# A two-layer decoder trunk on one core: one four-column tile of the base pool gets sixteen columns

## The chip, the cores and the metric

The kernel runs on one core of a Trainium2 chip. The metric is the device time of one execution in microseconds, as the median of several runs. A core has TensorE (PE; its weight loads are listed apart as PEld), VectorE (DVE), ScalarE (ACT), GpSimd (POOL) and SyncE (SP), which here only issues DMAs.

## The reference

The input is one sequence of 512 tokens of width 2048. Two layers follow each other, each with a modulated RMS norm in front and a gated residual add behind, and one RMS norm ends it:

```python
for i in range(DEPTH):                                   # DEPTH = 2
    mod = (c_act @ ada_w[i] + ada_b[i])[:, None, :]
    shift, scale, gate = jnp.split(mod, 3, axis=-1)
    h = rmsnorm(x, norm_g[i]) * (1.0 + scale) + shift
    if i % 2 == 0: y = retention_branch(h, positions, ...)   # 8 heads, dk 256, dv 512
    else:          y = mla_branch(h, positions, ...)         # 16 heads, ranks 512 and 512
    x = x + gate * y
return rmsnorm(x, final_norm_g)
```

The retention branch projects h to q, k (rotary), v and a gate g for 8 heads, forms decayed causal scores in chunks, normalises each head, multiplies by silu(g) and projects back. The attention branch projects h to two latent blocks of 512 (for queries, and for keys and values), one shared rotary key and a gate, expands the latents for 16 heads, does causal softmax attention, multiplies by silu(g) and projects back. All is float32.

## The kernel before

A product of float32 matrices is done as three matmuls on float32r parts: each operand x is split into a high part (a cast on ScalarE) and a low part x - high (a subtraction on VectorE), and high x high, high x low and low x high are added up in PSUM. Each matmul has a stationary operand of 128x128 and a moving operand of 128x512 or 128x256.

Tiles come from pools. The pool `base` lives through the whole kernel. It holds, in this order, the identity, mask and ones, a few columns of constants (`mhalf`, `rt`, `vcol` and six of the modulation), and then large tiles by tag, each tag with a fixed number of buffers: `big` (16 of 4096 bytes a partition), `small` (24 of 32 bytes), `k4` (8 of 4096), `k4b` (4 of 4096), `tmp` (6 of 2048), `raw` (3 of 4096), `whi` and `wlo` (3 of 4096 each). Behind these stand `qn_s` and two tiles of 64 bytes (`mod_c`). A tile takes its bytes of a partition rounded up to a multiple of 32. Behind `base` stands one inner pool at a time, each beginning at the same byte: `l0` in the first stage, `lp` in the stage of the retention heads' projections, `l1` in the retention and its output projection, `l2` in the attention layer.

Work goes in steps written out by hand (`Step`: load, prepare, multiply, follow); the order on each engine's queue is fixed by the program. DMAs of weights are issued on SP three units ahead.

The stage that most concerns the change is that of the heads 1 to 7. For each head the q and k rows are formed by `seven_rows_steps` (for heads 6 and 7 by plain steps), and values and gates by `seven_steps`: two products that share an input are done with seven half-products in the place of eight, over 8 units with four products and 8 units with three. Stationary is a block of h (`hT`, tag `big`) or of sums of its blocks (`sums`: 0 to 7 in `k4`, 8 to 11 in `k4b`, 12 to 15 in the inner pool). Moving is a part of the weights, 512 columns wide; in `seven_rows_steps` it is the other way round, and 256 columns wide. The names of parts: `vg_01o_h` is unit 1 of the first eight, its odd rows, high part; `vg_17e_l` is unit 7 of the second eight, even rows, low part.

Where raw weights and parts are put goes in turn:

```python
turns1 = turns(
    ((lambda: lpp, "own_r", 3), (lambda: base, "raw", 3)),
    ((lambda: lpp, ("own_h", "own_l"), 1), *3 * ((lambda: base, ("whi", "wlo"), 3),)),
)
```

So every second raw tile and every fourth pair of parts stand in `lp` (as `turns2` does in `l2`), the others in `base`. The odd parts of units 1, 3, 5 and 7 of the first eight and the even parts of units 1, 3, 5 and 7 of the second eight are those in `lp`. The product of `seven_steps` (lines 804 to 806 of the profile) is

```python
for b in range(2):
    a = form(n, u, b)
    PE.matmul(banks[b], a[0], w[0], start=first, stop=False, skip_group_check=True)
    PE.matmul(banks[b], a[0], w[1], start=False, stop=False, skip_group_check=True)
    PE.matmul(banks[b], a[1], w[0], start=False, stop=True, skip_group_check=True)
```

The latent rows of the second layer (`vgc_`) go through the same function with `l2` as the inner pool, and two of its gate blocks through `seven_rows_steps` (line 903). In the attention `pt`, the transposed probabilities in parts, stands in `l2` and is the moving operand of the value products. Transposes by TensorE (`yT` L1253, `pT` L1992, `y_ps` L2400) have the identity as one operand. DMAs that land in inner pools are every second raw tile, the modulation weights (`mod`, `aw`, `mod_gate`) and what the retention heads read back.

`qn_s` holds the four columns of one norm's gain, scaled by 192 to the power -1/2. It is written by one instruction of VectorE and read by four of ScalarE and four of VectorE.

Of the kernel before, what the change touches and what calls it, by code (L numbers as in the profile page):

```python
# [9 lines left out]
F32 = mybir.dt.float32  # L10
# [6 lines left out]
P = 128  # L17
T = 512
NT = T // P
# [30 lines left out]
def hybrid_trunk_kernel(  # L50
# [32 lines left out]
    base = ctx.enter_context(tc.tile_pool(name="base", bufs=1))  # L83
# [1654 lines left out]
            DVE.tensor_add(latent["q"][2 + b], m4[b], y_[b])  # L1738
            DVE.tensor_add(latent["kv"][2 + b], m5[b], y_[b])

    qn_s = base.tile([P, NT], F32, name="qn_s")

    def latent_norm(n):
        if n == "q":
# [726 lines left out]
```

## Time and profile before

| | before |
|---|---|
| three timed runs | 2156.14, 2157.33, 2159.07 us |
| median | 2157.33 us |
| the profiled execution: its span, first to last instruction | 2153.4 us |
| mean granted TensorE clock | 0.999 |
| HBM read, written | 417.96 MB, 43.00 MB |

The timed runs are whole executions; the profiled one is a further execution of which the span is known, 3.9 us under the median. A row of the views below names the line of the kernel, the engine, the operation and the tiles as out<-in with buffer numbers left out; x14 is a count. A matmul's duration in a row is longer than the distance between two matmuls' starts, since they are pipelined.

### The profile page before, as it was taken

The page shows a single profiled execution, that of the slowest core. Times are in us where ns is not written, and L with a number is a line of the kernel's source. Part 1 is how long each engine was busy: PE and PEld are TensorE (multiplying, and loading weights), DVE is VectorE, ACT ScalarE, POOL GpSimd, SP SyncE. Part 2 cuts the span into 40 slices and gives each one's busy share as a digit, 9 for nine tenths or more (in the row PEclk, how much of TensorE's full clock was granted, in tenths as well). Part 3 has the DMA queues.
Part 4 walks back from the last instruction along what each step waited for, and adds up shares of the span by engine and source line. Part 5 has one row for each costly group of instructions (what it writes and reads, how often), then busy time and mean ns, then how long its engine had stood idle before and what let it go on. Part 6 is the DMA issues. An engine that isn't in the chain of part 4 may idle for free.

```text
span 2153.4 us, 30041 instructions
## 1 busy us (share of the span) xinstructions
PE 2128.3 (99%) x11100; PEld 1822.8 (85%) x11100; DVE 1676.1 (78%) x2481; ACT 1057.1 (49%) x1604; POOL 106.8 (5%) x178
## 2 busy tenths in 40 slices
PE   7999999999999999999999999999999999999998
PEld 5888898988889888888888888898889989888887
DVE  7899788888878789766777787668978788886755
ACT  5764444444444444434344445345446565664434
POOL 1010000000000000000000000010001000000000
PEclk9999999999999999999999999999999999999999
DMA  9976686877777778765646567553556544346734
GB/s 382 401 278 196 224 273 225 274 239 259 255 258 255 230 235 281 246 206 168 242 158 233 188 215 248 166 171 113 166 178 208 182 137 145 118 135 220 243 109 137
DMA packets 229782, 462.96 MB, mean 215 GB/s; under 512 B 20817, under 2 KB 84337, under 8 KB 225793
## 3 DMA queue, kind: packets, MB, share of 16 engines
q1 hardware_dynamic: 217424, 421.85, 59.4%
q0 software_dynamic: 11920, 38.91, 4.6%
q8 instruction: 87, 1.43, 0.3%
q14 instruction: 61, 0.50, 0.1%
q10 hardware_dynamic: 290, 0.27, 0.0%
HBM read 417.96 MB, written 43.00 MB: 214 GB/s over the span
## 4 chain that ended last, share of the span: by engine, by line
PE 84%; DVE 6%; DMA 5%; issue 2%; ACT 2%; POOL 1%; SPq 0%; POOLq 0%; DVEq 0%; ACTq 0%
PE o L1385 9%; PE o L2307 4%; PE y L805 2%; PE y L806 2%; PE s L805 2%; PE y L804 2%; PE s L806 2%; PE x L806 2%; PE x L805 2%; PE s L804 2%; PE x L804 2%; PE x_qk L903 2%; PE y_qk L903 2%; PE s_qk L903 2%; PE qk L163 2%
## 5 line engine op out<-in xcount | busy, mean ns | idle before, releaser
L1385 PE MATMUL o<-o_h,o_whi 128*128 128x512 f32 (+1 forms) x496 | 192.3, 388 | 0.0
L1385 PE MATMUL o<-o_h,o_wlo 128*128 128x512 f32 (+1 forms) x496 | 191.5, 386 | 0.0
L1385 PE MATMUL o<-o_l,o_whi 128*128 128x512 f32 (+1 forms) x496 | 191.3, 386 | 0.0
L136 DVE TENSOR_TENSOR o_wlo<-o_r,o_whi 128x1024 fp32r<-128x1024 f32 x61 | 74.5, 1224 | 49.0 <-ACT o_whi L135 48.1
L1385 PEld LDWEIGHTS o<-o_h,o_wlo 128*128 128x128 f32 x496 | 93.2, 188 | 19.1 <-DVE o_wlo L136 0.4
L1385 PEld LDWEIGHTS o<-o_h,o_whi 128*128 128x128 f32 x496 | 93.2, 188 | 18.3
L1385 PEld LDWEIGHTS o<-o_l,o_whi 128*128 128x128 f32 x496 | 93.2, 188 | 18.2
L163 PE MATMUL qk<-hT,qk_l 128*128 128x512 f32 x192 | 74.9, 390 | 1.5 <-DVE qk_l L136 1.5
L135 ACT CAST o_whi<-o_r 128x1024 fp32r<-128x1024 f32 x61 | 63.5, 1051 | 25.0 <-PE o L1385 22.0
L356 DVE SCALAR_TENSOR_TENSOR aw<-aw,c_all 128x2048 f32<-128x2048 f32 (+1 forms) x35 | 73.2, 2103 | 2.5 <-DMA aw<-in_ada_t_dram 2.5
L161 PE MATMUL qk<-hT,qk_h 128*128 128x512 f32 x192 | 75.0, 391 | 0.0
L162 PE MATMUL qk<-hT,qk_h 128*128 128x512 f32 x192 | 74.7, 389 | 0.0
L1087 DVE SCALAR_TENSOR_TENSOR mod<-mod,c_odd 128x1024 f32<-128x1024 f32 x48 | 58.1, 1221 | 18.8 <-DMA mod<-in_ada_t_dram 18.8
L136 DVE TENSOR_TENSOR o_w_lo<-o_w_raw,o_w_hi 128x1024 fp32r<-128x1024 f32 x32 | 39.0, 1221 | 32.4 <-ACT o_w_hi L135 32.4
L1087 DVE SCALAR_TENSOR_TENSOR mod<-mod,c_bm 128x1024 f32<-128x1024 f32 x48 | 58.5, 1219 | 0.0
L2307 PE MATMUL o<-o_h,o_w_hi 128*128 128x512 f32 (+1 forms) x160 | 55.6, 348 | 0.0
L2307 PE MATMUL o<-o_h,o_w_lo 128*128 128x512 f32 (+1 forms) x160 | 55.5, 347 | 0.0
L2307 PE MATMUL o<-o_l,o_w_hi 128*128 128x512 f32 (+1 forms) x160 | 55.4, 347 | 0.0
L1240 ACT ACTIVATE yn<-y,nmr,gn_r 128x512 f32<-128x512 f32 x32 | 22.3, 778 | 62.0 <-DVE nmr L1234 62.0
L135 ACT CAST o_w_hi<-o_w_raw 128x1024 fp32r<-128x1024 f32 x32 | 33.5, 1051 | 36.0 <-PE o L2307 32.2
L135 ACT CAST o_h<-o_in 128x1024 fp32r<-128x1024 f32 x24 | 25.2, 1051 | 50.6 <-PE o L162 46.7
L161 PE MATMUL o<-o_h,o_w_hi 128*128 128x512 f32 x128 | 50.1, 391 | 0.0
(1607 smaller groups left out, 6896.6 us busy)
## 6 DMA issues: line engine op xcount, KB each, us to landing
mod<-in_ada_t_dram SPq DMA_DIRECT2D x96, 512.0 KB, 5.8
o_r<-in_ret_w_out_dram SPq DMA_DIRECT2D x64, 512.0 KB, 5.5
aw<-in_ada_t_dram SPq DMA_DIRECT2D x30, 1024.0 KB, 8.9
mod_gate<-in_ada_t_dram SPq DMA_DIRECT2D x32, 512.0 KB, 5.1
o_w_raw<-in_mla_w_out_dram SPq DMA_DIRECT2D x32, 512.0 KB, 4.1
qk_r<-in_ret_w_in_dram SPq DMA_DIRECT2D x48, 256.0 KB, 3.1
qk_r<-qk_d SPq DMA_DIRECT2D x32, 256.0 KB, 6.0
v_r<-v_d SPq DMA_DIRECT2D x32, 256.0 KB, 6.2
```

Of the source, the lines that this page charges most:

```text
L135: ACT.copy(hi, src)
L136: DVE.tensor_sub(lo, src, hi.bitcast(F32))
L161: PE.matmul(o, lhs[0], rhs[0], start=first and not seeded, stop=False, skip_group_check=seeded)
L162: PE.matmul(o, lhs[0], rhs[1], start=False, stop=False, skip_group_check=seeded)
L163: return PE.matmul(o, lhs[1], rhs[0], start=False, stop=last, skip_group_check=seeded)
L804: PE.matmul(banks[b], a[0], w[0], start=first, stop=False, skip_group_check=True)
L805: PE.matmul(banks[b], a[0], w[1], start=False, stop=False, skip_group_check=True)
L806: PE.matmul(banks[b], a[1], w[0], start=False, stop=True, skip_group_check=True)
L903: PE.matmul(o, w[wp][:, i, b * P : (b + 1) * P], a[ap], start=first and i + b + k == 0, stop=k == 2, skip_group_check=True,)
L1087: DVE.scalar_tensor_tensor(out=aw, in0=aw, scalar=1.0, in1=silu_c[j], op0=ALU.mult, op1=ALU.mult, accum_out=mc[:, j, b : b + 1],)
L1385: PE.matmul(o, w[i][:, ki, c0 + b * P : c0 + (b + 1) * P], a[j], start=first and i + j == 0, stop=last and i == 1, skip_group_check=True,)
L2307: PE.matmul(banks2[b][:, cols], w[0][i][:, 0, b * P : (b + 1) * P], o2_moving(w, u, cols)[j], start=u + i + j == 0, stop=u == KD - 1 and i ...
```

## The change

`qn_s` is allocated with 16 columns in the place of 4, and its first four columns are used. It takes 64 bytes of a partition, where it took 16, rounded up to 32. What stands behind it, the two `mod_c` tiles and all inner pools, begins 32 bytes later. No instruction is added, removed or moved.

```diff
-    qn_s = base.tile([P, NT], F32, name="qn_s")
+    qn_s = base.tile([P, 16], F32, name="qn_s")[:, :NT]
```

## The prediction

> **What bounds the kernel now.** I read the page first, then the windows view by stage, then the view of one line (L804) and of single tiles, then the timeline of TensorE.
>
> ```profile
> span 2153.4 us, 30041 instructions
> ...
> PE 2128.3 (99%) x11100; PEld 1822.8 (85%) x11100; DVE 1676.1 (78%) x2481; ACT 1057.1 (49%) x1604; POOL 106.8 (5%) x178
> ...
> PE   7999999999999999999999999999999999999998
> ...
> DMA  9976686877777778765646567553556544346734
> ...
> PE 84%; DVE 6%; DMA 5%; issue 2%; ACT 2%; POOL 1%; SPq 0%; POOLq 0%; DVEq 0%; ACTq 0%
> ```
>
> TensorE is the bound: 2128.3 of 2153.4 us busy, 84% of the chain of waits. A change that adds and removes no instruction can only matter here if TensorE's own instructions get longer or shorter. The profiled execution has a span of 2153.4 us; the median of the three timed runs is 2157.33 us (2156.14 to 2159.07), so I put 3.9 us outside the span and carry a change of the span over to the median one to one. What a measurement of this kernel can tell from no change is about 0.2%, that is 4.3 us.
>
> ```profile
> core 0: us, PE busy (x) PEld busy (x) DVE busy (x) ACT busy (x) POOL busy (x), PEclk, DMA share, GB/s
> ...
> 201.00:284.00 83.00, 83.00 (x365) 67.97 (x364) 65.75 (x82) 39.52 (x48) 4.30 (x8) 1.00 0.75 241
> ...
> 440.00:560.00 120.00, 120.00 (x691) 105.60 (x690) 100.61 (x130) 55.10 (x66) 8.28 (x15) 1.00 0.77 254
> ...
> 1555.00:1625.00 70.00, 70.00 (x310) 57.29 (x309) 50.87 (x62) 31.37 (x38) 0.00 (x0) 1.00 0.61 195
> ```
>
> In the stages that form the retention heads' values and gates (201 to 908 us) and the latent rows (1555 to 1624 us) TensorE has no idle time at all, at full clock, while VectorE is at 0.73 to 0.84 and the DMA engines at 0.61 to 0.77. Whatever a matmul gains or loses in these stages shows in the end.
>
> **Where the tiles begin.** This is arithmetic on the program, not on the chip. A pool lays its tiles one behind another, each rounded up to 32 bytes of a partition. Ahead of the first large tile of the base pool stand, from byte 4224 (a multiple of 64), three tiles of 512, two of 32 (16 rounded up), vcol of 736 and six of 64 bytes: 2720 bytes, so the tag big begins at byte 6944, remainder 32 of 64. The other large tags follow in multiples of 64 and have the same remainder. qn_s (16 bytes, rounded to 32) stands behind them, so the small tiles after it and the inner pools (l0, lp, l1, l2) begin at remainder 0: byte 171712 for the first. With 64 bytes for qn_s everything behind it moves by 32 bytes, and all large tiles stand at remainder 32. [...]
>
> **What the trace shows of it.** In seven_steps the moving operand is a part of the weights. Every fourth pair of parts is taken from the inner pool (own_h, own_l), the others from the base pool (whi, wlo). So one line holds both kinds. The columns are ns min/median/max over the seven heads.
>
> ```profile
> L804 PE MATMUL x<-vg_01e_h,hT x14: 389/389/389, 211.8 to 836.7; 128*128 128x512 f32 x14
> ...
> L804 PE MATMUL z<-vg_01o_h,hT x14: 394/396/398, 214.5 to 839.4; 128*128 128x512 f32 x14
> ...
> L804 PE MATMUL x<-vg_02e_h,hT x14: 389/390/393, 217.3 to 842.2; 128*128 128x512 f32 x14
> ...
> L804 PE MATMUL z<-vg_02o_h,hT x14: 389/389/389, 220.1 to 844.9; 128*128 128x512 f32 x14
> ...
> L804 PE MATMUL s<-vg_06e_h,sums x14: 394/394/394, 240.7 to 865.6; 128*128 128x512 f32 x14
> ...
> L804 PE MATMUL y<-vg_17e_h,sums x14: 387/388/390, 282.2 to 907.0; 128*128 128x512 f32 x14
> ```
>
> vg_01e, vg_02o and hT are base tiles: 389 ns, all fourteen times. vg_01o is an inner tile: 396. vg_02e is a base tile again, but follows right behind the inner one and needs a few matmuls to get back. In s<-vg_06e_h,sums the moving operand is a base tile and the stationary one (sums 12, in lp) an inner one: 394. In y<-vg_17e_h,sums both are inner tiles: 387 to 390, like base tiles that have just been disturbed. So it is the mixing of remainders 0 and 32 that goes with the longer time, in whichever operand. The timeline shows how far apart matmuls start:
>
> ```profile
> 323.73 0.40 PE L804 MATMUL x<-vg_00e_h,hT 128*128 128x512 f32 x1
> ...
> 326.05 0.39 PE L805 MATMUL s<-vg_00e_l,sums 128*128 128x512 f32 x1
> ...
> 329.22 0.39 PE L804 MATMUL x<-vg_01e_h,hT 128*128 128x512 f32 x1
> ...
> 331.94 0.40 PE L804 MATMUL z<-vg_01o_h,hT 128*128 128x512 f32 x1
> ...
> 334.75 0.39 PE L804 MATMUL x<-vg_02e_h,hT 128*128 128x512 f32 x1
> ...
> 400.97 0.40 PE L903 MATMUL x_qk<-hT,qk_00e_h 128*128 128x256 f32 x2
> ```
>
> Twelve matmuls of base tiles take 331.94 - 329.22 = 2.72 us, 226.7 ns each. The twelve with vg_01o take 334.75 - 331.94 = 2.81 us, 234 ns each: 7 ns more, as in the durations.
>
> **The change part by part.** It removes, adds and moves no instruction, DMA or wait; no queue is passed.
>
> Matmuls of 512 columns in seven_steps: one head has 8 units of 4 products and 8 of 3, each of 2 blocks by 3 passes, so (32 + 24) x 6 = 336 matmuls. From 323.73 to 400.97 they take 77.24 us; at 226.7 ns each they would take 76.17 us. The excess is 1.07 us a head. Of it 108 matmuls have one or two inner operands (66 in the first eight units, 42 in the second), at 6 to 7 ns; the rest are base matmuls just behind them. After the change I take all of them at 226.7 ns, except the first ten of a head, which come from the 256-column matmuls of L903 out of step: 323.73 to 326.05, 232 ns each, an excess of 0.05 us that stays. Gain 1.02 us a head. Seven heads and the latent rows (the same function and steps; I take the same excess) make 8 x 1.02 = 8.2 us, all on TensorE without a pause, hidden by nothing. What would be late next is VectorE at 0.84, so nothing waits.
>
> Matmuls of 256 columns (the q and k heads and two gate blocks, seven_rows_steps):
>
> ```profile
> L903 PE MATMUL y_qk<-sums,qk_01o_h x32: 278/280/286, 293.6 to 647.1; 128*128 128x256 f32 x32
> L903 PE MATMUL s_qk<-sums,qk_02e_h x32: 283/283/283, 296.5 to 650.0; 128*128 128x256 f32 x32
> ...
> L903 PE MATMUL y_qk<-sums,qk_03o_h x32: 278/282/283, 302.2 to 655.7; 128*128 128x256 f32 x32
> L903 PE MATMUL s_qk<-sums,qk_03e_h x32: 277/280/282, 303.7 to 657.1; 128*128 128x256 f32 x32
> ```
>
> Here mixing goes the other way: 283 ns with base tiles (qk_02e), 280 to 282 with an inner operand (qk_01o, qk_03o, qk_03e). By the code 96 of a pass's 336 have one, six passes, some 580 matmuls. Matched, I price them at 283: 2 ns each, 1.2 us lost; the bounds are 0 (they keep their time) and 3 ns, 1.7 us.
>
> The attention's value products take pt from the inner pool as moving operand: three 512-column matmuls for each of 16 heads, 48 x 7 ns = 0.3 us at most. I leave it out of the sum and put it in the range.
>
> Transposes read ident, which stands at remainder 0 ahead of all this, with a base tile (x2, L2400) or an inner one (yn, L1253) as the other operand:
>
> ```profile
> L2400 PE MATMUL y_ps<-ident,x x32: 272/272/306, 2139.5 to 2144.5; 128*128 128x128 f32 x32
> ...
> L1253 PE MATMUL yT<-ident,yn x128: 270/272/283, 993.6 to 1364.2; 128*128 128x128 f32 x128
> ```
>
> 272 ns either way: the change, which makes the second like the first, costs nothing here.
>
> VectorE and ScalarE (both vg_01o and vg_02o are read raw from the inner pool, written to inner and to base tiles):
>
> ```profile
> L838 ACT CAST vg_01o_h<-vg_01o_r x7: 1050/1054/1054, 208.0 to 834.6; 128x1024 fp32r<-128x1024 f32 x7
> L839 DVE TENSOR_TENSOR vg_01o_l<-vg_01o_r,vg_01o_h x7: 1219/1226/1226, 209.3 to 835.7; 128x1024 fp32r<-128x1024 f32 x7
> ...
> L838 ACT CAST vg_02o_h<-vg_02o_r x7: 1048/1050/1051, 212.7 to 840.3; 128x1024 fp32r<-128x1024 f32 x7
> L839 DVE TENSOR_TENSOR vg_02o_l<-vg_02o_r,vg_02o_h x7: 1224/1226/1226, 213.8 to 841.4; 128x1024 fp32r<-128x1024 f32 x7
> ```
>
> 1226 against 1226 and 1054 against 1050: the remainder is worth at most 4 ns in 1050, beside work at 0.84 of the stage or less. Nothing.
>
> DMAs that land in inner tiles (mod) against base tiles (o_r), the same 512 KB:
>
> ```profile
> mod<-in_ada_t_dram SPq DMA_DIRECT2D x96, 512.0 KB, 5.8
> o_r<-in_ret_w_out_dram SPq DMA_DIRECT2D x64, 512.0 KB, 5.5
> ```
>
> The base tiles, which have the remainder that all will have, are landed on no slower; between -0.3 us and nothing for a transfer, with TensorE busy beside it. I take 0.
>
> Sum: -8.2 + 1.2 = -7.0 us on the span: 2146.4 us, and 2157.3 - 7.0 = 2150.3 us for the time (-0.32%).
>
> **The rivals.** First, no change: the longer matmuls have another cause than the remainder. Every inner tile stands at remainder 0 and also above byte 171712, so the rows can't part the remainder from the place in the memory; if it is the place, vg_01o stays at 396 and the time at 2157.3 us. [...] Against this rival also stands y<-vg_17e_h,sums: both operands lie high up, and yet it falls to 387, below the 394 of a mixed pair. Chance 0.14.
>
> Second, slower: what counts is the remainder of 128 bytes. The base tiles stand at 32 of 128, the inner ones at 64 now and at 96 after, so the distance would grow from 32 to 64 bytes, the largest there is, and mixed matmuls would stay out of step and be worse off. If the 864 mixed ones (108 in each of eight passes) go from their present 394 to 396 to the longest that one of them takes now, the 403 at the end of this row,
>
> ```profile
> L804 PE MATMUL y<-vg_06o_h,sums x14: 396/399/403, 243.4 to 868.3; 128*128 128x512 f32 x14
> ```
>
> that is 8 ns each, 6.9 us, and 2164.2 us. It decides from 5 ns on, where 864 x 5 = 4.3 us can be told from nothing; below that it reads as no change. No tile of this kernel shows a distance of 64, so nothing excludes it; against it speaks a little that distances of 256 bytes do no harm: hT (6944, remainder 288 of 512) and the base parts (146976, remainder 32 of 512) are in step at 389. Chance 0.12.
>
> [...]
>
> **How the numbers follow.** The forecast (matched remainders bring all to 226.7 ns) has 0.72, no change 0.14, slower 0.12, something else 0.02, on either side. The forecast's own range is 2147 to 2154: the gain is 8.5 us with the attention's part and without the loss at 256 columns (2148.8), 4.1 us if those lose 1.7 and the base matmuls behind the mixed ones stay out of step (1.07 less 0.05 for the first ten and 0.72 for 108 mixed ones at 6.7 ns leaves 0.3 us a head, 2.4 us in eight passes; 2153.2). The three runs scatter by 1.5 us, which comes on top. For 8 in 10 it has to take in the case of no change with its scatter: 2147.0 to 2158.8. Faster by over 0.2% 0.73, within 0.2% 0.15, slower by over 0.2% 0.12.
>
> **What would show it.** Right: in the view of L804, vg_01o_h, vg_03o_h, s<-vg_06e_h,sums and y<-vg_17e_h,sums all at 389 and vg_02e_h at 389/389/389; a head from its first matmul to the next stage in 76.2 us instead of 77.24; qk_01o_h and qk_03e_h at 283; 30041 instructions as before. Wrong: vg_01o_h still at 394 or more (then it was the place, or 128 bytes), or these rows at 389 and a stage with new idle time of TensorE (then it was given back).

## The result, and the profile after

The change makes the kernel a little faster: 2152.83 us median of 20 runs (2150.89 to 2155.93) against 2157.95 us of 20 runs before (2155.44 to 2159.81), a ratio of 0.9978 with a 95% interval of 0.9972 to 0.9984. That is 5.1 us. The forecast was 7.0 us, and its sign and its range hold; its mechanism doesn't, as the rows show, so that the range was met in part by luck.

The page of the kernel after, the lines that answer to those shown of before:

```profile
span 2151.3 us, 30041 instructions
...
PE 2126.0 (99%) x11100; PEld 1821.6 (85%) x11100; DVE 1675.4 (78%) x2481; ACT 1056.3 (49%) x1604; POOL 106.7 (5%) x178
...
PE 84%; DVE 6%; DMA 4%; issue 2%; ACT 2%; POOL 1%; SPq 0%; DVEq 0%; POOLq 0%; ACTq 0%
```

TensorE's busy time falls by 2.3 us, VectorE's and ScalarE's by less than 1 us. The span falls by only 2.1 us, less than the medians. The rest is scatter of the two profiled executions. A profiled run of the kernel after has a time of 2153.12 us with a span of 2151.3, so 1.8 us lie outside the span and not 3.9: the execution whose profile the prediction read was itself about 3 us under the median of its kernel. One place of it is seen in the windows of the second layer's output projection (columns as in the windows of the prediction), before:

```profile
2011.00:2058.00 47.00, 46.98 (x207) 38.59 (x206) 39.46 (x53) 21.82 (x26) 0.00 (x0) 1.00 0.67 222
```

and after, with the view of TensorE's waits in the same stretch (us in total, times, longest):

```profile
2011.00:2058.00 47.00, 46.17 (x201) 37.28 (x200) 37.49 (x49) 19.83 (x23) 0.00 (x0) 1.00 0.64 214
```

```profile
PE o L162 <- DVE o_l L136: 0.7, 2, 0.4
```

The execution before has TensorE busy for 46.98 of 47 us there, the one after for 46.17. In the profiles of the experiments below it is 45.0 to 47.0, and 45.2 in a second profile of the kernel after: how long TensorE waits there for the low parts of the projection's input (o_l) differs from execution to execution. So less can be read from two spans than from the stages.

The rows of seven_steps after, ns min/median/max, in the view of L804 and then in views of single tiles:

```profile
L804 PE MATMUL x<-vg_01e_h,hT x14: 389/389/389, 212.1 to 833.7; 128*128 128x512 f32 x14
...
L804 PE MATMUL z<-vg_01o_h,hT x14: 394/394/394, 214.9 to 836.4; 128*128 128x512 f32 x14
...
L804 PE MATMUL x<-vg_02e_h,hT x14: 388/392/395, 217.7 to 839.2; 128*128 128x512 f32 x14
```

```profile
L804 PE MATMUL s<-vg_06e_h,sums x14: 392/392/392, 241.0 to 862.6; 128*128 128x512 f32 x14
...
L804 PE MATMUL y<-vg_17e_h,sums x14: 389/390/391, 282.2 to 903.7; 128*128 128x512 f32 x14
```

vg_01o, the moving operand from the inner pool, is not at 389. It went from 394/396/398 to 394 fourteen times: not much shorter, but steady. s<-vg_06e_h,sums, with an inner stationary operand, went from 394 to 392. Between the first and the last vg_01e_h lie 621.6 us after (212.1 to 833.7) and 624.9 before (211.8 to 836.7): 3.3 us of the gain are made here, over six passes with the q and k stages between them. The rows of seven_rows_steps (L903) show the surprise:

```profile
L903 PE MATMUL y_qk<-sums,qk_01o_h x32: 276/276/276, 293.5 to 645.0; 128*128 128x256 f32 x32
L903 PE MATMUL s_qk<-sums,qk_02e_h x32: 283/283/283, 296.3 to 647.9; 128*128 128x256 f32 x32
L903 PE MATMUL y_qk<-sums,qk_03o_h x32: 278/282/283, 302.1 to 653.6; 128*128 128x256 f32 x32
L903 PE MATMUL s_qk<-sums,qk_03e_h x32: 281/281/281, 303.5 to 655.0; 128*128 128x256 f32 x32
```

The 256-column matmuls of an inner stationary operand and a base moving one (qk_01o) fell from 278/280/286 to 276, 7 ns under those of base tiles alone (qk_02e), which stayed at 283. The timeline of one head:

```profile
323.45 0.39 PE L804 MATMUL x<-vg_00e_h,hT 128*128 128x512 f32 x1
...
328.94 0.39 PE L804 MATMUL x<-vg_01e_h,hT 128*128 128x512 f32 x1
...
331.65 0.39 PE L804 MATMUL z<-vg_01o_h,hT 128*128 128x512 f32 x1
...
334.45 0.39 PE L804 MATMUL x<-vg_02e_h,hT 128*128 128x512 f32 x1
...
400.31 0.40 PE L903 MATMUL x_qk<-hT,qk_00e_h 128*128 128x256 f32 x2
```

Twelve matmuls with vg_01o take 334.45 - 331.65 = 2.80 us, 233.3 ns each, where base tiles take 226 (331.65 - 328.94 = 2.71 us). The whole pass takes 76.86 us in the place of 77.24, not the 76.2 that the forecast needs.

**A sum over all matmuls.** Laid beside the program's addresses, the starts of the trace give a price list. For each float32r matmul I take the time to the next one's start, leave out those with a pause behind them (over 260 ns at 512 columns, 139 at 256), and take off the shortest steady spacing, 226.7 ns at 512 columns and 113.3 at 256 (what vg_01e and qk_01o have after). The sum of what is over is what the layout costs. The rows are sorted by the distance, the start of the moving operand less that of the stationary one, modulo 256 bytes; "inner moving" is a pair of which the moving operand alone stands in an inner pool, and pairs of two inner tiles are in the row of distance 0:

| distance | before: count, mean ns, us over | after: count, mean ns, us over |
|---|---|---|
| 512 columns, 0 | 6318, 227.5, 5.2 | 6307, 227.3, 3.8 |
| 512, inner moving | 528 at 160, 233.6, 3.7 | 528 at 192, 233.3, 3.5 |
| 512, inner stationary | 288 at 96, 233.4, 1.9 | 288 at 64, 229.6, 0.8 |
| 256 columns, 0 | 2541, 119.7, 16.2 | 2541, 119.7, 16.2 |
| 256, inner moving | 216 at 160, 117.5, 0.9 | 216 at 192, 116.6, 0.7 |
| 256, inner stationary | 312 at 96, 119.5, 1.9 | 312 at 64, 114.0, 0.2 |
| sum of us over | 29.8 | 25.3 |

So -2.6 us at 512 columns, -1.9 us at 256, together -4.5 us beside the measured -5.1.

### The profile page after: what moved, and what is told of

Its sections match the earlier page's. It is cut to its first block, busy times and chain, and to the rows that moved or that the text cites. A ratio compares the mean times of both kernels' runs of the same rounds, so it can differ in the third digit from the quotient of the medians.

```text
span 2151.3 us, 30041 instructions
## 1 busy us (share of the span) xinstructions
PE 2126.0 (99%) x11100; PEld 1821.6 (85%) x11100; DVE 1675.4 (78%) x2481; ACT 1056.3 (49%) x1604; POOL 106.7 (5%) x178
## 4 chain that ended last, share of the span: by engine, by line
PE 84%; DVE 6%; DMA 4%; issue 2%; ACT 2%; POOL 1%; SPq 0%; DVEq 0%; POOLq 0%; ACTq 0%
PE o L1385 11%; PE o L2307 4%; PE y L805 2%; PE y L804 2%; PE y L806 2%; PE s L805 2%; PE x L805 2%; PE s L804 2%; PE x L804 2%; PE s L806 2%; PE x L806 2%; PE x_qk L903 2%; PE s_qk L903 2%; PE y_qk L903 2%; PE qk L163 2%
## 5 line engine op out<-in xcount | busy, mean ns | idle before, releaser
L162 PE MATMUL o<-o_l,o_w_hi 128*128 128x512 f32 x128 | 50.2, 392 | 0.8 <-DVE o_l L136 0.7
```

The source lines that it names most:

```text
L162: PE.matmul(o, lhs[0], rhs[1], start=False, stop=False, skip_group_check=seeded)
```

## The experiments

Two theories stood at first. **Theory A**: what counts is the distance between the two operands' starts, with a period of more than 64 bytes (128 or 256); at 0 a 512-column matmul is at its shortest. **Theory B**, the first rival on record: the place, whatever stands behind the base pool costs more. **Rival C** came with the second set: a tile's own remainder, not the distance. The theory on record (a remainder of 64 bytes, matched, brings all to 389) has fallen by the row of vg_01o_h. Every kernel below differs from the kernel before by the lines shown; times are medians, beside the kernel before on the same chip.

### Inner pools moved by 96, 64, 160 and 128 bytes

The first matches base and inner tiles modulo 256 (32 and 32):

```diff
-    qn_s = base.tile([P, NT], F32, name="qn_s")
+    qn_s = base.tile([P, 32], F32, name="qn_s")[:, :NT]
```

> qn_s with 32 columns (128 bytes): all behind it moves by 96 bytes, so inner and base tiles begin at the same remainder of 128, and of 256, bytes. Theory A (the distance between the two operands' remainders of 128 or 256 bytes decides): the 512-column matmuls with an inner operand start 226.7 ns apart and z<-vg_01o_h reads 389, the 8.1 us that they and those behind them take over that before the change all but go; the 256-column ones with an inner operand go to the 120 ns and 283 ns of base tiles, about 0.9 us more than before the change. Sum -6.7 us against the kernel before, about 2151.2 us, 1.7 us under the changed kernel. Theory B (the place: whatever stands behind the base pool costs as moving operand): z<-vg_01o_h stays at 394 or more, time 2153 to 2158 us.

Measured: 2149.59 us (5 runs) against 2157.84, ratio 0.9965 (0.9953 to 0.9978). Its matmuls of L804 and L903, in views of tiles:

```profile
L804 PE MATMUL z<-vg_01o_h,hT x14: 389/389/389, 214.6 to 833.6; 128*128 128x512 f32 x14
...
L804 PE MATMUL x<-vg_02e_h,hT x14: 389/389/389, 217.4 to 836.4; 128*128 128x512 f32 x14
...
L804 PE MATMUL s<-vg_06e_h,sums x14: 389/389/389, 240.5 to 859.5; 128*128 128x512 f32 x14
...
L804 PE MATMUL y<-vg_17e_h,sums x14: 389/389/389, 281.3 to 900.3; 128*128 128x512 f32 x14
```

```profile
L903 PE MATMUL y_qk<-sums,qk_01o_h x32: 283/283/283, 292.7 to 643.4; 128*128 128x256 f32 x32
...
L903 PE MATMUL s_qk<-sums,qk_03e_h x32: 283/283/283, 302.8 to 653.5; 128*128 128x256 f32 x32
```

These are, row by row, the rows that the prediction wanted to see of the change, with inner tiles that stand 64 bytes further up than the change puts them. A head's pass on its timeline takes 399.13 - 322.94 = 76.19 us:

```profile
322.94 0.40 PE L804 MATMUL x<-vg_00e_h,hT 128*128 128x512 f32 x1
...
399.13 0.40 PE L903 MATMUL x_qk<-hT,qk_00e_h 128*128 128x256 f32 x2
```

Theory B says 394 here, and has fallen.

The next has 24 columns (inner tiles at 0 of 256, distances 224 and 32):

```diff
-    qn_s = base.tile([P, NT], F32, name="qn_s")
+    qn_s = base.tile([P, 24], F32, name="qn_s")[:, :NT]
```

> qn_s with 24 columns (96 bytes): inner tiles move by 64 bytes, remainder 0 of 128, 32 bytes away from the base tiles' 32 on the other side. Theory A: a distance of 32 again, so as before the change: 512-column matmuls with an inner operand 231 to 240 ns apart and unsteady, 256-column ones at 117 to 120 ns, 2157 to 2159 us. The theory on record (remainder of 64 bytes) says the same here. Theory B: as the changed kernel, 2153 us.

Measured: 2154.65 us, ratio 0.9987 (0.9978 to 0.9995), 3.2 us under the kernel before. 2157 to 2159 was expected: a miss. vg_01o_h is at 396/396/397 and qk_01o_h at 277/279/281. The sum of us over is 27.9, which accounts for 1.9 us of the 3.2. With a period of 128 the distances (96 and 32) would be those of before with the roles exchanged; that they cost another sum doesn't yet decide it.

48 columns move the inner tiles by 160 bytes, to 96 of 256; the distances of the changed kernel modulo 128, and its two distances modulo 256 with the roles exchanged (64 moving, 192 stationary):

```diff
-    qn_s = base.tile([P, NT], F32, name="qn_s")
+    qn_s = base.tile([P, 48], F32, name="qn_s")[:, :NT]
```

> qn_s with 48 columns (192 bytes): inner tiles move by 160 bytes, the same remainder of 128 as in the changed kernel (distance 64), another of 256. If 128 bytes is the period: the same as the changed kernel, 2152.8 us within 0.1%, z<-vg_01o_h at 394 without scatter (233.3 ns apart), qk_01o_h at 113.3 ns apart. If 256 bytes is the period: the two roles change places, a moving inner operand then costs what a stationary one costs now (512 columns 229.6 ns apart on the mean, 256 columns 114) and a stationary one what a moving one costs now (233.3 and 117); by the counts of each (480 moving, 288 stationary at 512 columns; 216 and 312 at 256) -1.8 + 1.1 - 0.6 + 0.9 = -0.4 us, the same in time but another view of L804. Theory B: no change against the changed kernel in either.

Measured: 2156.07 us, ratio 0.9994 (0.9985 to 1.0003), 3.2 us over the changed kernel although both have the same distance modulo 128. So 128 bytes is not the period:

```profile
L804 PE MATMUL z<-vg_01o_h,hT x14: 394/396/398, 214.7 to 838.5; 128*128 128x512 f32 x14
...
L804 PE MATMUL x<-vg_02e_h,hT x14: 397/397/397, 217.4 to 841.3; 128*128 128x512 f32 x14
...
L903 PE MATMUL y_qk<-sums,qk_01o_h x32: 281/281/281, 293.7 to 646.5; 128*128 128x256 f32 x32
```

qk_01o_h is at 281 where the changed kernel has 276. What the expectation for a period of 256 says of the means came true in kind: the inner moving operand (now at 64) starts 231.3 ns apart and the inner stationary one (now at 192) 233.2; at 256 columns 115.9 and 118.0. Its time did not (-0.4 us against the changed kernel was worked out, +3.2 measured). The base matmuls behind the inner ones, which that sum left out, are out of step longer, that is, take longer to come back to their steady spacing: vg_02e_h is at 397 with hT and still at 393/395/398 with sums, where the changed kernel is back at 389, and the row of distance 0 has 5.6 us over in the place of 3.8. And the 256-column matmuls with one inner operand have 1.1 us more over than in the changed kernel, where +0.3 was worked out.

And 40 columns, a move by 128 (inner at 64 of 256, distances 32 and 224):

```diff
-    qn_s = base.tile([P, NT], F32, name="qn_s")
+    qn_s = base.tile([P, 40], F32, name="qn_s")[:, :NT]
```

> qn_s with 40 columns (160 bytes): inner tiles move by 128 bytes, the same remainder of 128 as in the kernel before. If 128 bytes is the period (theory A): the same as the kernel before, 2157 to 2159 us. If the period is 256 bytes: distances of 32 and 224 in the place of 160 and 96, still no multiple of 64, so unsteady, 2155 to 2160 us. Theory B: as the changed kernel, 2153 us.

Measured: 2155.98 us, ratio 0.9993 (0.9984 to 1.0002), unclear against the kernel before. The time is in the range for a period of 256 and 1 us under the one for 128. The row tells more: modulo 128 the distances are those of before, and vg_01o_h, 394/396/398 there, is at

```profile
L804 PE MATMUL z<-vg_01o_h,hT x14: 397/398/399, 214.5 to 838.5; 128*128 128x512 f32 x14
```

### All tiles moved, and the weights alone

Distance or own remainder? mhalf stands ahead of the large base tiles. Wider, it moves them by 32 bytes; with qn_s at 32 columns all tiles are then at 64 of 256:

```diff
-    mhalf = base.tile([P, NT], F32, name="mhalf")
+    mhalf = base.tile([P, 16], F32, name="mhalf")[:, :NT]
...
-    qn_s = base.tile([P, NT], F32, name="qn_s")
+    qn_s = base.tile([P, 32], F32, name="qn_s")[:, :NT]
```

> mhalf with 16 columns moves the large base tiles by 32 bytes, to remainder 64 of 256; qn_s with 32 columns brings the inner pools to 64 of 256 as well. Theory A (only the distance between the two operands counts, with a period of 256 bytes): as with all tiles at 32 of 256, 2149.6 us within 0.1%, z<-vg_01o_h at 389, qk_00e at 283. Rival C (a remainder of its own counts, 32 of 64 being the good one for 512 columns): base matmuls too change, z<-vg_00o_h leaves 389, and the time is at least that of the kernel before, 2158 us.

Measured: 2150.44 us against 2157.43, ratio 0.9969 (0.9957 to 0.9980).

```profile
L804 PE MATMUL z<-vg_00o_h,hT x14: 389/389/389, 209.2 to 828.2; 128*128 128x512 f32 x14
...
L804 PE MATMUL z<-vg_01o_h,hT x14: 389/389/389, 214.7 to 833.7; 128*128 128x512 f32 x14
...
L903 PE MATMUL x_qk<-hT,qk_00e_h x32: 278/283/283, 282.7 to 633.4; 128*128 128x256 f32 x32
```

Then mhalf alone, so that all tiles move by 32 bytes and every distance stays:

```diff
-    mhalf = base.tile([P, NT], F32, name="mhalf")
+    mhalf = base.tile([P, 16], F32, name="mhalf")[:, :NT]
```

> mhalf with 16 columns and nothing else: base and inner tiles all move by 32 bytes, each distance as in the kernel before, each remainder another. Theory A: the same as the kernel before, 2157.8 us within 0.1%, z<-vg_01o_h at 394 to 398, z<-vg_00o_h at 389. Rival C: the matmuls of base tiles alone change, several us either way.

Measured: 2157.27 us, ratio 1.0001 (0.9992 to 1.0009).

```profile
L804 PE MATMUL z<-vg_00o_h,hT x14: 389/389/389, 209.1 to 833.9; 128*128 128x512 f32 x14
...
L804 PE MATMUL z<-vg_01o_h,hT x14: 394/396/398, 214.5 to 839.4; 128*128 128x512 f32 x14
...
L804 PE MATMUL y<-vg_17e_h,sums x14: 387/388/390, 282.1 to 907.0; 128*128 128x512 f32 x14
```

These are the durations of the kernel before, to the nanosecond, unsteadiness included; between 184 and 960 us all 4032 matmul starts of the two traces stay within 1 ns of one offset. As far as this move goes only the distance counts, and rival C has fallen. The place is not tested by it, since the inner tiles stay behind the base pool.

If so, the effect must also reach the base pool's own matmuls, once its weights stand at a distance. Here qn_s is taken ahead of whi, with 192 bytes; whi and wlo go to 224 of 256, inner tiles to 96:

```diff
+    ahead = []
...
+            if tags[0][0] == "whi" and not ahead:
+                ahead.append(base.tile([P, 48], F32, name="qn_s"))
             hl = [base.tile([P, 2, cn], F32R, tag=t, bufs=n, name=f"{kind}0_{u}_{t}{i}") for i, (t, n) in enumerate(tags)]
...
-    qn_s = base.tile([P, NT], F32, name="qn_s")
+    qn_s = ahead[0][:, :NT]
```

> 192 bytes ahead of whi (qn_s lies in them): whi and wlo go to remainder 224 of 256, the base tiles ahead of them stay at 32, the inner pools go to 96 (as in the kernel moved by 160). So nearly all matmuls have a distance. Theory A, with the starts measured at these distances (moving less stationary, of 256): 512 columns with 192: 233.3 ns, with 64: 229 to 231; 256 columns with 64: 113.3 to 118. By the counts in the trace 2016 matmuls of 512 columns have whi or wlo moving (192, +6.6 ns: +13.4 us), 3480 have them stationary (64, +2.3 to 4.6 ns: +8 to +16 us), 1704 of 256 columns have them stationary (64, -1.9 to -6.6 ns: -3.2 to -11.3 us). Sum +10 to +26 us against the kernel before: 2168 to 2184 us, and z<-vg_01e_h at 394, qk_00e at 276 to 281. Theory B (place): whi and wlo stay below the inner pools, no change, 2158 us.

Measured: 2163.39 us, ratio 1.0027 (1.0017 to 1.0037): slower by 6.0 us. The statements of L804 and L903 are L807 and L906 here:

```profile
L807 PE MATMUL x<-vg_01e_h,hT x14: 393/396/398, 213.7 to 839.8; 128*128 128x512 f32 x14
...
L906 PE MATMUL x_qk<-hT,qk_00e_h x32: 279/280/282, 286.1 to 639.3; 128*128 128x256 f32 x32
```

The base tiles now have both the longer 512-column matmuls (396 for 389) and the shorter 256-column ones (280 for 283). Theory B, no change, falls once more. The time lies below the 2168 to 2184 worked out. The terms, from the starts: 512 columns at 192 have 12.6 us over (13.4 expected) and at 64 9.7 us (8 to 16 expected); all of 256 columns 11.7 in the place of 19.1 (-7.4, -3.2 to -11.3 expected). What the sum left out: the 512-column matmuls still at distance 0 have 1.5 us over in the place of 5.2. All together 37.4 against 29.8 us, +7.6 beside the measured +6.0.

This trace also speaks on a period of 512 bytes, which no run was made for. Among its base pairs, distances of 64 and of 320 bytes cost the same (229.0 and 229.0 ns at 512 columns, 116.2 and 116.1 at 256), and so do 192 and 448 (233.0 and 232.9 at 512 columns), in groups of 696 to 2488 matmuls. In smaller groups the means differ more, up to 4.7 ns in the changed kernel at 256 columns (168 at 192 against 48 at 448), which stand between other neighbours.

### One operand alone

Only own_h and own_l of the retention heads' stage move by 96 bytes, to 32 of 256; sums and the latent rows stay as before:

```diff
+            if tags[0] == "own_h":
+                n_ = shape[1] * shape[2] if len(shape) == 3 else shape[1]
+                hi = pool().tile([P, 24 + 1024], F32R, tag="own_h", bufs=1, name=f"{name}_h")[:, 24 : 24 + n_]
+                if len(shape) == 3:
+                    hi = hi.rearrange("p (a n) -> p a n", a=shape[1])
+                return [hi, pool().tile(shape, F32R, tag="own_l", bufs=1, name=f"{name}_l")]
             return [pool().tile(shape, F32R, tag=tag, bufs=bufs, name=f"{name}_{p}") for p, tag in zip("hl", tags)]
```

> As the kernel before, but own_h and own_l of the retention heads' stage alone are moved by 96 bytes, to remainder 32 of 256; sums 12 to 15 and all else stay. Theory A: z<-vg_01o_h and vg_02e_h behind it go to 389, s<-vg_06e_h,sums stays at 394, y<-vg_17e_h,sums becomes a mixed pair and goes from 387 to some 394. In us over seven heads: the moving ones -3.40 x 7/8 = -3.0, those behind them about half of 2.31 x 7/8 = -1.0, pairs of two inner tiles +0.2, 256 columns 0 to +0.2: -3.7 against the kernel before, 2154.1 us. Theory B: no change, 2158 us.

Measured: 2152.89 us against 2157.43, ratio 0.9982 (0.9973 to 0.9991), 4.5 us where 3.7 were expected. L810 is the statement of L804:

```profile
L810 PE MATMUL z<-vg_01o_h,hT x14: 389/389/389, 214.7 to 836.0; 128*128 128x512 f32 x14
...
L810 PE MATMUL x<-vg_02e_h,hT x14: 389/389/389, 217.4 to 838.8; 128*128 128x512 f32 x14
L810 PE MATMUL s<-vg_06e_h,sums x14: 394/394/394, 240.5 to 861.9; 128*128 128x512 f32 x14
...
L810 PE MATMUL y<-vg_17e_h,sums x14: 394/394/394, 281.8 to 903.1; 128*128 128x512 f32 x14
```

All four rows as expected: the moving operand is cured, the stationary one isn't, and the pair of two inner tiles, 387 to 390 before, has become a mixed one at 394. A tile that was moved to the remainder of the base pool made one of its own matmuls longer: it is the pair.

### The two best side by side

The changed kernel (qn_s with 16 columns) and the one moved by 96 bytes (32 columns), on one chip:

> The changed kernel (inner pools moved by 32 bytes) on the same chip as the next one. Theory A: 4.5 us under the kernel before, from its own trace's starts, 2153 us; vg_01o_h at 394.

> Inner pools moved by 96 bytes, beside the changed kernel. Theory A, from the starts in the traces (excess over the shortest pitch 22.0 us here, 25.3 us in the changed kernel, 29.8 us before): 3.3 us under the changed kernel, 7.8 us under the kernel before, 2150 us.

Measured: 2152.54 us, ratio 0.9980 (0.9971 to 0.9989), and 2149.48 us, ratio 0.9967 (0.9955 to 0.9979), both against 2157.43. vg_01o_h is at 394/394/395 in the first and 389/389/389 in the second. With 2149.59 and 2150.44 us in the runs above, three sets have a full match 2.1 to 3.4 us below the change's 2152.5 and 2152.8; the two intervals still overlap between 0.9971 and 0.9979, but of the six runs of the second only the longest (2151.78 us) reaches the shortest of the first's eleven (2151.74).

Each kernel in one table, with its first set of runs. "Over" is the sum of the table above, from each kernel's own trace:

| kernel | distances, moving / stationary inner | us over | against before | measured against before |
|---|---|---|---|---|
| before | 160 / 96 | 29.8 | | |
| changed (moved by 32) | 192 / 64 | 25.3 | -4.5 | -5.1 |
| moved by 64 | 224 / 32 | 27.9 | -1.9 | -3.2 |
| moved by 96 | 0 / 0 | 22.0 | -7.8 | -8.3 |
| moved by 128 | 32 / 224 | 28.7 | -1.1 | -1.9 |
| moved by 160 | 64 / 192 | 28.3 | -1.5 | -1.8 |
| all at 64 of 256 | 0 / 0 | 22.1 | -7.7 | -7.0 |
| all moved by 32 | 160 / 96 | 30.1 | +0.3 | -0.2 |
| weights at 224 | most at 192 or 64 | 37.4 | +7.6 | +6.0 |
| own parts alone | 0 / 96 | 25.9 | -3.9 | -4.5 |

The starts account for every kernel's time to within 1.6 us, over a spread of 14 us, and each sum lies within the interval of its kernel's measured ratio.

## Why the prediction was right, and where it was wrong

**The bound** was right: TensorE without a pause in these stages, and what its matmuls gain shows in the time (4.5 us by the starts, 5.1 measured). No new wait took it back: from 440 to 560 us it is busy for all 120 us after, as before.

**What counts** was wrong. The step that failed is "after the change I take all of them at 226.7 ns": the 480 matmuls of seven_steps with an inner moving and a base stationary operand start 233.3 ns apart. The prediction took the remainder of 64 bytes, because the trace of before had only two kinds of pairs, 0 and 32 of 64, and matched pairs were short. The same rows allowed any period up to 256, since all base tiles share their remainder of 256 (32). The prediction even had the row for it, hT and the parts at 288 and 32 of 512 in step at 389, and used it only as an argument against the second rival. The experiments give 256: the same distance modulo 128 gave two times (2152.8 and 2156.1), and the pairs at distances of 0 and 256 of 512, as those of 64 and 320, are alike. By its own sign of being wrong, vg_01o_h at 394, the mechanism on record fell.

**The sum for 512 columns**, -8.2 us, is near the price of a full match: the kernel moved by 96 bytes has 2.0 us over where 10.8 are over before, -8.8. The change pays -2.6. It makes an inner stationary operand cheaper (233.4 to 229.6 ns), a moving one hardly (233.6 to 233.3), and the matmuls at distance 0 lose less in all (5.2 to 3.8 us over).

**The sum for 256 columns** had the wrong sign: +1.2 us forecast, -1.9 found. It too is right for a full match (+1.0: 19.1 us over before, 20.0 moved by 96). At the distance that the change gives, 64, the 312 with an inner stationary operand start 114.0 ns apart in the place of 119.5. With the 216 of an inner moving operand these are 528 pairs of unlike tiles, where the prediction had some 580.

So two misses, +5.6 and -3.1 us, made -4.5 out of -7.0. They partly cancel, which is luck, and the forecast of "faster" was right by a mechanism that wasn't the one on record. Even the second rival, that a period over 64 bytes counts, was nearer to it, but not its price: at a distance of 64 of 128 the kernel is better than at 32, not worse (25.3 against 29.8 us over). Its 864 matmuls take in the 12 of each pass whose operands both stand in the inner pool; 96 a pass, 768 in all, are pairs of unlike tiles, which makes its 6.9 us 6.1.

**What was put at nothing** stayed there. The transposes have 272 ns as before, DVE and ACT their busy times to within 0.8 us; the modulation weights that land in moved tiles (mod) take 5.8 us from issue to landing in both pages.

**The first rival**, the place, was refuted by the match at 96 bytes (inner tiles at 389), by the weights at 224 (base tiles at 396) and by the own parts alone (vg_17e_h, still an inner tile with an inner partner, from 387 to 394). What the spacing goes with here is the distance between the two operands: 226.9 to 233.6 ns at 512 columns and 114.0 to 119.9 at 256 on the mean. The runs do not show where in TensorE or the memory the time goes. In the view of L804 after, a weight load begins some 0.2 us before its matmul, and by the timeline as the matmul ahead of it starts (both at 213.28 us):

```profile
L804 PEld LDWEIGHTS s<-vg_01e_h,sums x14: 187/188/188, 213.3 to 834.8; 128*128 128x128 f32 x14
L804 PE MATMUL s<-vg_01e_h,sums x14: 389/389/389, 213.5 to 835.1; 128*128 128x512 f32 x14
```

The starts tell which two operands meet. Where three or more steady matmuls of base tiles (226 or 227 ns) go over to an inner moving operand, the last of them keeps its 226 or 227 ns in all 57 cases of the kernel before, and the first with the inner operand takes 234 or 235. Where they go over to an inner stationary operand, the last matmul of base tiles, itself at distance 0, is already long: 235 to 237 ns in all 17 such cases of the kernel moved by 64 bytes, all 23 of that moved by 128 and all 14 of the own parts alone. As far as these cases show, the spacing goes by the moving operand of one matmul and the stationary one of the next, whose load begins with it. Why it does so is not shown. Nor is it why matmuls back at distance 0 need several more to get into step (in the kernel before three behind vg_01o, 230 to 233 ns from start to start).

**The time outside the span**, 3.9 us by the prediction, is 1.8. The profiled execution was a short one, 2.7 us under the median of its kernel; a span from one profile should not be set against a median from others to get such a difference.

## What to carry to other kernels

Where TensorE is the bound, let the tiles that meet in 512-column matmuls begin at the same remainder of 256 bytes of a partition, not of 64: a pad of 96 bytes gave 8 us of 2158 here, the change's 32 gave 5. Before you take a period from rows, list which periods the rows allow, and move everything by one step (no change expected) as well as one side alone. Look at each shape by itself: 512 columns are at their shortest here at a distance of 0 (226.9 to 228.4 ns), 256 columns at 64 (114.0 to 116.1).

## What the runs showed of the hardware

The spacing of float32r matmuls with 128x128 weights, by the distance between moving and stationary start modulo 256 bytes (means, with the matmuls that are getting into step):

| distance | 0 | 32 | 64 | 96 | 128 | 160 | 192 | 224 |
|---|---|---|---|---|---|---|---|---|
| 512 columns, ns | 226.9 to 228.4 | 233.0 to 233.6 | 229.1 to 231.3 | 233.4 to 233.5 | 232.9 | 232.8 to 233.6 | 233.0 to 233.3 | 232.6 to 233.6 |
| 256 columns, ns | 119.5 to 119.9 | 117.2 to 117.5 | 114.0 to 116.1 | 119.4 to 119.5 | 118.7 | 117.5 to 117.8 | 116.0 to 118.0 | 118.2 |

A matched pair, the shortest at 512 columns, is the longest at 256, where most pairs sit at 120 ns, 6.7 over the 113.3 of qk_01o after the change. The 3069 such matmuls of the kernel moved by 96 bytes have 20 us over. To have 0 for the one shape and 64 for the other, the weights of the q and k rows would need tiles of their own; this was not tried.
